# A softmax that streams 128 row groups through one core: the last four of six 15-row loads issued as two 30-row loads

## Chip, cores, metric

The kernel runs on one core of a Trainium2 chip. The metric is device time in microseconds (us), median of three runs. One core has five engines with their own instruction streams (TensorE, VectorE, ScalarE, GpSimd, SyncE; in the profile PE, DVE, ACT, POOL, SP) and 16 DMA engines that all DMA queues share. A DMA that is issued by SP, ACT or POOL goes to a queue of that issuer; the profile calls SP's queue q1, ACT's q10 and POOL's q0.

## The reference

```python
x: (16, 1024, 512) float32
x_scaled = x / 2.0
exp_x = np.exp(x_scaled - max(x_scaled, axis=-1))
return exp_x / sum(exp_x, axis=-1)        # softmax over the last 512
```

16384 rows of 512 floats are read once and written once: 33.55 MB in, 33.55 MB out.

## The kernel before

The rows are taken as 128 row groups ("rows" from here on): a row is 512 floats on each of 128 partitions, 0.262 MB. The 128 rows are cut into ten tiles, listed in `TILES` (L10) as (rows, place in the arena): 3, 5, and eight times 15. The tile numbers 0 to 9 are positions in this list. A tile of r rows is laid out so that partition p holds r neighbouring rows of DRAM: with r = 15 that is one run of 30720 bytes per partition.

The data live in one SBUF buffer, `arena` (L49), of 98 rows. Tiles 0 to 7 fill it (3 + 5 + 6 x 15 = 98). Tiles 8 and 9 reuse the places of rows 0 to 29: tile 8 those of tiles 0, 1 and 2 (the first 15 rows), tile 9 those of tiles 2 and 3. `LATE` (L14) writes this down: the load of tile 8 waits for the stores of tiles 0, 1 and 2, the load of tile 9 for that of tile 3.

Everything is done in place, and each engine runs through the tiles in order:

- **Loads.** SP loads tile 0, ACT tile 1 (`early`, L155), ACT then tiles 2 to 7 one behind the other with no wait between them (`loads`, L159). POOL loads tiles 8 and 9 (L178 to L181): it waits until the exponentials of all rows below row 83 are done (`TURN`, L22; that is the end of tile 6), then for the stores named in `LATE`.
- **Release to ACT.** PE waits for each tile's load in order and raises `s_go` by the number of chunks in the tile (L195, L196). A chunk is 5 rows, the first one 3.
- **Exponentials.** ACT takes one unit of `s_go` for a chunk (L142), then runs one ACTIVATE per row: exp(x/2) with the sum of the row into `stats` (L206, L275). The maximum is not subtracted; a check of the sums at the end (L182 to L192) sets a flag, and only if a sum is outside of its limits does a slow path recompute everything (`rounds`, L144).
- **Normalising.** DVE takes the reciprocal of the sums (L168) and multiplies the tile by it (L171): one pair of instructions for each 15-row tile, for the last tile one per 5 rows. `upto[t]` is the number of multiplications after which tile t is ready.
- **Stores.** SP stores the tiles in order (L213 to L216), each after its multiplication (L135). Tile 1 (`SPREAD`, L20) is stored in three DMAs (`pieces`, L116): four of its five rows on 128 partitions (8192 bytes each), the fifth row on 126 partitions (2048 bytes each), and the fifth row on the last two partitions. Before the store of tile 2, SP waits until all pieces of tiles 0 and 1 have landed (L215): 64 on the semaphore `s_home[8]`.

So the order of transfers is set by three queues (ACT's loads, SP's stores, POOL's two late loads), each in the order of issue, and by how the DMA engines share themselves between the queues.

Of the kernel before, what the change touches and what calls it, by code (L numbers as in the profile page):

```python
# [10 lines left out]
    (3, 0), (5, 3), (15, 8), (15, 23), (15, 38), (15, 53), (15, 68), (15, 83), (15, 0), (15, 15),  # L11
]

LATE = {8: (0, 1, 2), 9: (3,)}  # L14
ARENA = 98

HEAD = [3]
# [2 lines left out]
SPREAD = 1  # L20
# [8 lines left out]
def kernel(  # L29
# [5 lines left out]
    nc = tc.nc  # L35
# [6 lines left out]
    xf = x.flatten_outer_dims()  # L42
    of = out.flatten_outer_dims()
    N, D = xf.shape
    P = nc.NUM_PARTITIONS
# [14 lines left out]
    tiles, base = [], 0  # L60
# [2 lines left out]
        tiles.append((base, r, at))  # L63
        base += r

    def dram(ap, t):
        b, r, _ = tiles[t]
        return ap[b * P : (b + r) * P].rearrange("(p r) d -> p r d", r=r)

    def sb(t):  # L70
        _, r, at = tiles[t]
        return arena[:, at : at + r, :]

    straight = sum(HEAD)
# [3 lines left out]
    owner = [max(t for t, (b, _, _) in enumerate(tiles) if b <= s) for s in starts]  # L78
# [9 lines left out]
            pairs.append([k])  # L88
    upto = [1 + max(j for j, ks in enumerate(pairs) if owner[ks[0]] == t) for t in range(len(tiles))]

    ld = [nc.alloc_semaphore(f"ld{t}") for t in range(len(tiles))]
    s_home = {t: nc.alloc_semaphore(f"s_home{t}") for t in LATE}
    s_near = nc.alloc_semaphore("s_near")
    s_end = nc.alloc_semaphore("s_end")
    s_exp = nc.alloc_semaphore("s_exp")
    s_go = nc.alloc_semaphore("s_go")
    s_rec = nc.alloc_semaphore("s_rec")
    s_mul = nc.alloc_semaphore("s_mul")
# [11 lines left out]
    g_rec = nc.alloc_semaphore("g_rec")  # L110
    g_mul = nc.alloc_semaphore("g_mul")

    def load(eng, t):
        eng.dma_start(out=sb(t), in_=dram(xf, t)).then_inc(ld[t], 16)  # L114

    def pieces(t):  # L116
        r = tiles[t][1]
        if t == SPREAD:
            return [(0, P, 0, r - 1), (0, 126, r - 1, r), (126, P, r - 1, r)]
        return [(0, P, 0, r)]  # L120

    stored_by = {u: s_home[t] for t, us in LATE.items() for u in us}
    for t, (_, r, at) in enumerate(tiles):
        over = {u for u, (_, ru, au) in enumerate(tiles[:t]) if at < au + ru and au < at + r}
        assert over <= {u for v, us in LATE.items() if v <= t for u in us}

    def landings(ts):
        return 16 * sum(len(pieces(t)) for t in ts)

    near = len(tiles) - 2  # L130
    sem_of = {**stored_by, near: s_near}
    at_end = landings(t for t in range(len(tiles)) if t not in sem_of)

    def store(eng, t):
        eng.wait_ge(s_mul, upto[t])  # L135
        for p, q, lo, hi in pieces(t):
            eng.dma_start(
                out=dram(of, t)[p:q, lo:hi], in_=sb(t)[p:q, lo:hi]
            ).then_inc(sem_of.get(t, s_end), 16)

    def take(eng, sem, n):
        eng.wait_ge(sem, n).then_inc(sem, -n)  # L142

    def rounds(eng, body):  # L144


        i = eng.alloc_register("general")
        eng.wait_ge(s_near, 16)
        eng.wait_ge(s_flag, 1)
        eng.reg_load(i, flag[0:1, 0:1])  # L150
        with eng.While(lambda: eng.snap(i, min_val=0, max_val=1) < 1):
            body()
            eng.reg_add(i, i, 1)

    def early():  # L155
        load(nc.sync, 0)
        load(nc.scalar, 1)

    def loads():  # L159
        for t in range(2, min(LATE)):  # L160
            load(nc.scalar, t)

    def program():

        for j, ks in enumerate(pairs):
            b, c = starts[ks[0]], sum(sizes[k] for k in ks)
            a = b % ARENA
            nc.vector.reciprocal(  # L168
                out=recip[:, b : b + c], in_=stats[:, b : b + c]
            )._wait_ge(s_exp, ks[-1] + 1).then_inc(s_rec, 1)  # L170
            nc.vector.tensor_mul(  # L171
                out=arena[:, a : a + c],
                in0=arena[:, a : a + c],
                in1=recip[:, b : b + c].unsqueeze(2).to_broadcast([P, c, D]),
            )._wait_ge(s_rec, j + 1).then_inc(s_mul, 1)

        nc.gpsimd.memset(ones[:, :], 1.0).then_inc(s_ones, 1)  # L177
        nc.gpsimd.wait_ge(s_exp, starts.index(TURN))  # L178
        for t, us in LATE.items():
            nc.gpsimd.wait_ge(s_home[t], landings(us))  # L180
            load(nc.gpsimd, t)  # L181
        nc.gpsimd.tensor_scalar(  # L182
            out=inside[:, :], in0=stats[:, :], scalar1=LO, scalar2=HI,
            op0=Alu.max, op1=Alu.min,
        )._wait_ge(s_exp, len(sizes)).then_inc(s_cnt, 1)
        nc.vector.scalar_tensor_tensor(  # L186
            out=inside[:, :], in0=inside[:, :], scalar=1.0, in1=stats[:, :],
            op0=Alu.mult, op1=Alu.is_equal, accum_out=count[:, :],
        )._wait_ge(s_cnt, 1).then_inc(s_cnt, 1)
        nc.vector.tensor_scalar(  # L190
            out=flag[:, :], in0=total[:, :], scalar1=float(N), scalar2=None, op0=Alu.is_ge,
        )._wait_ge(s_tot, 1).then_inc(s_flag, 1)  # L192


        for t in range(len(tiles)):  # L195
            nc.tensor.wait_ge(ld[t], 16).then_inc(s_go, owner.count(t))  # L196
        nc.tensor.wait_ge(s_ones, 1)
        nc.tensor.matmul(  # L198
            total[:, :], lhsT=count[:, :], rhs=ones[:, :], start=True, stop=True
        )._wait_ge(s_cnt, 2).then_inc(s_tot, 1)  # L200

        nc.scalar.preload_act_table(Exp)  # L202
        for k, c in enumerate(HEAD):
            take(nc.scalar, s_go, 1)
            for b in range(starts[k], starts[k] + c):
                ins = nc.scalar.activation(  # L206
                    out=arena[:, b], in_=arena[:, b], func=Exp, scale=0.5,
                    accum_out=stats[:, b : b + 1],
                )
            ins.then_inc(s_exp, 1)  # L210
        exponentials(straight, n_rows)

        for t in range(len(tiles)):  # L213
            if t == SPREAD + 1:
                nc.sync.wait_ge(s_home[min(LATE)], landings(range(t)))  # L215
            store(nc.sync, t)  # L216

        x_g = xf.rearrange("(t p r) d -> t p r d", p=P, r=G)  # L220
        o_g = of.rearrange("(t p r) d -> t p r d", p=P, r=G)
        data = arena[:, 0:G]

        def vector():
            for i in range(n_rows // G):
                nc.vector.reduce_max(
                    out=g_max[:, :], in_=data, axis=mybir.AxisListType.X, negate=True
                )._wait_ge(g_go, i + 1).then_inc(g_top, 1)
                nc.vector.reduce_sum(
                    out=g_sum[:, :], in_=data, axis=mybir.AxisListType.X  # L230
                )._wait_ge(g_exp, i + 1).then_inc(g_add, 1)
                nc.vector.reciprocal(
                    out=g_sum[:, :], in_=g_sum[:, :]
                )._wait_ge(g_add, i + 1).then_inc(g_rec, 1)

        def scalar():
            for i in range(n_rows // G):
                nc.scalar.activation(out=data, in_=data, func=Exp, scale=0.5)._wait_ge(
                    g_sub, i + 1
                ).then_inc(g_exp, 1)  # L240

        def gpsimd():
            nc.gpsimd.wait_ge(s_end, at_end)
            for i in range(n_rows // G):
                nc.gpsimd.dma_start(out=data, in_=x_g[i]).then_inc(g_ld, 16)
                nc.gpsimd.wait_ge(g_ld, 16 * (i + 1)).then_inc(g_go, 1)
                nc.gpsimd.tensor_add(
                    out=data, in0=data, in1=g_max[:, :].unsqueeze(2).to_broadcast([P, G, D])
                )._wait_ge(g_top, i + 1).then_inc(g_sub, 1)
                nc.gpsimd.tensor_mul(  # L250
                    out=data, in0=data, in1=g_sum[:, :].unsqueeze(2).to_broadcast([P, G, D])
                )._wait_ge(g_rec, i + 1).then_inc(g_mul, 1)
                nc.gpsimd.wait_ge(g_mul, i + 1)
                nc.gpsimd.dma_start(out=o_g[i], in_=data).then_inc(g_st, 16)
                nc.gpsimd.wait_ge(g_st, 16 * (i + 1))

        rounds(nc.vector, vector)
        rounds(nc.scalar, scalar)
        rounds(nc.gpsimd, gpsimd)
        nc.sync.wait_ge(s_near, 16)  # L260
        nc.sync.wait_ge(s_end, at_end)
# [26 lines left out]
    first = list(entry.instructions)  # L288
    at = next(k for k, i in enumerate(head) if type(i).__name__ == "InstDrain")
    entry.instructions = head[:at] + first + head[at:]  # L290
    act = []
    entry.instructions = list(entry.instructions) + [i for i in jumps if i not in act]
    nc.switch_body(here, parent=None, valid_engines=[i.engine for i in jumps])
    loads()
    program()


# [28 lines left out]
```

## Time and profile before

| | us |
|---|---|
| median of 3 runs (159.81 to 159.98) | 159.98 |
| the profiled execution | 159.75 |
| its span in the profile | 158.4 |
| ACT busy, of the span | 80.6 |
| DVE busy, of the span | 73.2 |
| last DVE instruction ends | 129.4 |
| bytes moved | 67.11 MB, 424 GB/s over the span |

The profiled execution took 0.23 us less than the median of the runs and 1.35 us more than its own span. All times in the text below are microseconds from the span's start. The profile also records single DMA packets: on this kernel one packet is the run of one partition in a DMA (30720 bytes for a 15-row tile), and each DMA has 8 of them on each of the 16 engines, followed on each engine by a 4-byte packet that reports completion.

### The profile page before, as it was taken

What the parts mean: (1) busy time and instruction counts of PE and PEld (TensorE: products, weight loads), DVE (VectorE), ACT (ScalarE), POOL (GpSimd) and SP (SyncE); (2) the same over time, 40 slices, a digit from 0 to 9 for tenths busy, and PEclk for the clock granted to TensorE, in tenths of its full rate; (3) what the DMA queues carried; (4) which work ended last, traced back from release to release, by engine and by line L of the source; (5) the groups of instructions that cost most, each with busy time, mean ns of one, the idle gap of its engine ahead of it and who ended that gap; (6) DMA issues with size and microseconds to landing.
All of it is one profiled execution on the core that took longest, in us unless ns stands there. A gap on an engine that the chain in (4) does not pass through costs nothing. (4 is left out here: it accounts for less than half of the span.)

```text
span 158.4 us, 658 instructions
## 1 busy us (share of the span) xinstructions
PE 0.2 (0%) x2; PEld 0.1 (0%) x2; DVE 73.2 (46%) x27; ACT 80.6 (51%) x257; POOL 2.2 (1%) x8
## 2 busy tenths in 40 slices
PE   0000000000000000000000000000000000000000
PEld 0000000000000000000000000000000000000000
DVE  0066000992994979903970029808927960000000
ACT  0780399598899980795005971991059700000000
POOL 0000000000000000001000010000000100000000
DMA  7999998999999999999898989898989898989896
GB/s 270 469 411 383 461 439 357 446 470 412 395 502 389 442 427 427 442 411 458 388 481 380 489 380 489 380 489 380 489 372 496 372 489 380 489 380 489 380 481 264
DMA packets 3024, 67.11 MB, mean 424 GB/s; under 512 B 336, under 2 KB 336, under 8 KB 720
## 3 DMA queue, kind: packets, MB, share of 16 engines
q1 hardware_dynamic: 1728, 34.34, 50.7%
q10 hardware_dynamic: 1008, 24.90, 37.0%
q0 software_dynamic: 288, 7.86, 11.5%
HBM read 33.55 MB, written 33.55 MB: 424 GB/s over the span
## 5 line engine op out<-in xcount | busy, mean ns | idle before, releaser
L275 ACT ACTIVATE arena<-arena x125 | 76.7, 615 | 40.2 <-ACTq L142 40.2
L171 DVE TENSOR_TENSOR arena<-arena,recip 128x7680 f32<-128x7680 f32 (+2 forms) x12 | 70.2, 5847 | 0.4
L168 DVE RECIPROCAL recip<-stats 128x15 f32<-128x15 f32 (+2 forms) x12 | 2.7, 224 | 55.5 <-ACT arena L275 47.3
L275 ACT ACTIVATION_READ_ACCUMULATOR arena<-arena x125 | 23.4, 187 | 0.0
L202 ACT ACT_TABLE_LOAD x1 | 1.3, 1283 | 5.0 <-issue 5.0
L114 POOL DMA_DIRECT2D arena<-in_x_dram x2 | 1.3, 631 | 90.3 <-ACT arena L275 72.3
L206 ACT ACTIVATE arena<-arena 128x512 f32<-128x512 f32 x3 | 1.9, 618 | 0.0
L182 POOL TENSOR_SCALAR inside<-stats 128x128 f32<-128x128 f32 x1 | 0.6, 631 | 32.6 <-ACT arena L275 32.6
L206 ACT ACTIVATION_READ_ACCUMULATOR arena<-arena 128x1 f32 x3 | 0.6, 185 | 0.0
L198 PE MATMUL total<-ones,count 128*1 128x1 f32 x2 | 0.2, 164 | 129.1 <-DVE inside L186 129.1
L186 DVE SCALAR_TENSOR_TENSOR inside<-inside,stats 128x128 f32<-128x128 f32 x1 | 0.3, 284 | 0.0
L190 DVE TENSOR_SCALAR flag<-total 1x1 int32<-1x1 f32 x1 | 0.1, 147 | 0.3 <-PE total L198 0.3
L198 PEld LDWEIGHTS total<-ones,count 128*1 128x1 f32 x2 | 0.1, 80 | 129.1 <-DVE inside L186 129.1
L177 POOL MEMSET ones<- 128x1 f32 x1 | 0.1, 99 | 1.1 <-POOLq L37 1.1
L310 POOL MEMSET const-float32-0.0<- 128x1 f32 x1 | 0.1, 105 | 0.2 <-issue 0.2
L310 POOL MEMSET const-bfloat16-1.0<- 128x1 bf16 x1 | 0.1, 108 | 0.0
L310 POOL MEMSET const-uint8-127<- 128x1 uint8 x1 | 0.1, 108 | 0.0
L310 POOL MEMSET const-float32-1.0<- 128x1 f32 x1 | 0.1, 105 | 0.0
L186 DVE DVE_READ_ACCUMULATOR inside<-inside,stats 128x1 f32 x1 | 0.1, 83 | 0.0
## 6 DMA issues: line engine op xcount, KB each, us to landing
out_dram<-arena SPq DMA_DIRECT2D x8, 3840.0 KB, 42.9
arena<-in_x_dram ACTq DMA_DIRECT2D x6, 3840.0 KB, 41.7
arena<-in_x_dram POOLq DMA_DIRECT2D x2, 3840.0 KB, 23.7
arena<-in_x_dram ACTq DMA_DIRECT2D x1, 1280.0 KB, 7.3
out_dram<-arena SPq DMA_DIRECT2D x1, 1024.0 KB
arena<-in_x_dram SPq DMA_DIRECT2D x1, 768.0 KB, 5.9
out_dram<-arena SPq DMA_DIRECT2D x1, 768.0 KB
out_dram<-arena SPq DMA_DIRECT2D x1, 252.0 KB
```

The source lines that it names most:

```text
L114: eng.dma_start(out=sb(t), in_=dram(xf, t)).then_inc(ld[t], 16)
L168: nc.vector.reciprocal(out=recip[:, b : b + c], in_=stats[:, b : b + c])._wait_ge(s_exp, ks[-1] + 1).then_inc(s_rec, 1)
L171: nc.vector.tensor_mul(out=arena[:, a : a + c], in0=arena[:, a : a + c], in1=recip[:, b : b + c].unsqueeze(2).to_broadcast([P, c, D]),)._w ...
L177: nc.gpsimd.memset(ones[:, :], 1.0).then_inc(s_ones, 1)
L182: nc.gpsimd.tensor_scalar(out=inside[:, :], in0=stats[:, :], scalar1=LO, scalar2=HI, op0=Alu.max, op1=Alu.min,)._wait_ge(s_exp, len(sizes) ...
L186: nc.vector.scalar_tensor_tensor(out=inside[:, :], in0=inside[:, :], scalar=1.0, in1=stats[:, :], op0=Alu.mult, op1=Alu.is_equal, accum_ou ...
L190: nc.vector.tensor_scalar(out=flag[:, :], in0=total[:, :], scalar1=float(N), scalar2=None, op0=Alu.is_ge,)._wait_ge(s_tot, 1).then_inc(s_f ...
L198: nc.tensor.matmul(total[:, :], lhsT=count[:, :], rhs=ones[:, :], start=True, stop=True)._wait_ge(s_cnt, 2).then_inc(s_tot, 1)
L202: nc.scalar.preload_act_table(Exp)
L206: ins = nc.scalar.activation(out=arena[:, b], in_=arena[:, b], func=Exp, scale=0.5, accum_out=stats[:, b : b + 1],)
L275: ins = nc.scalar.activation(out=data, in_=data, func=Exp, scale=0.5, accum_out=stats[:, r : n_rows - E + 1 + r][:, bass.ds(now, 1)],)
L310: nc = _bacc.Bacc("TRN2", target_bir_lowering=False, num_devices=1)
```

## The change

The list of tiles stays, but what one load and one store cover is now listed apart from it. `LOADS` puts tiles 4 and 5 into one load and tiles 6 and 7 into one load; `STORES` has one store per tile as before. In a 30-row load, partition p holds 30 neighbouring rows of DRAM: one run of 61440 bytes, of which tile 4 is the first half and tile 5 the second. The stores of tiles 4 to 7 still move 15 rows, 30720 bytes per partition, now with a step of 61440 bytes in DRAM between partitions.

With it, the semaphores `ld` are one per load; PE waits for a load and releases all chunks of both its tiles at once (six instead of three). ACT issues five loads instead of seven. `LATE` is renumbered by loads (tile 8 is load 6, tile 9 load 7); what the late loads wait for, the chunks, the multiplications, the pieces of tile 1 and the order on SP stay as they were.

```diff
-LATE = {8: (0, 1, 2), 9: (3,)}
+LOADS = [(0,), (1,), (2,), (3,), (4, 5), (6, 7), (8,), (9,)]
+STORES = [(0,), (1,), (2,), (3,), (4,), (5,), (6,), (7,), (8,), (9,)]
+
+LATE = {6: (0, 1, 2), 7: (3,)}
...
-    def dram(ap, t):
-        b, r, _ = tiles[t]
-        return ap[b * P : (b + r) * P].rearrange("(p r) d -> p r d", r=r)
-
-    def sb(t):
-        _, r, at = tiles[t]
+    def span(ts):
+        assert all(tiles[u][2] == tiles[t][2] + tiles[t][1] for t, u in zip(ts, ts[1:]))
+        return tiles[ts[0]][0], sum(tiles[t][1] for t in ts), tiles[ts[0]][2]
...
+    blocks = [span(ts) for ts in LOADS]
+
+    def dram(ap, ts):
+        b, r, _ = span(ts)
+        first, rows, _ = next(blocks[k] for k, us in enumerate(LOADS) if ts[0] in us)
+        assert first <= b and b + r <= first + rows
+        block = ap[first * P : (first + rows) * P].rearrange("(p r) d -> p r d", r=rows)
+        return block[:, b - first : b - first + r]
+
+    def sb(ts):
+        _, r, at = span(ts)
         return arena[:, at : at + r, :]
...
-    def load(eng, t):
-        eng.dma_start(out=sb(t), in_=dram(xf, t)).then_inc(ld[t], 16)
...
+    def load(eng, k):
+        eng.dma_start(out=sb(LOADS[k]), in_=dram(xf, LOADS[k])).then_inc(ld[k], 16)
...
-    def store(eng, t):
-        eng.wait_ge(s_mul, upto[t])
-        for p, q, lo, hi in pieces(t):
+    def store(eng, j):
+        ts = STORES[j]
+        eng.wait_ge(s_mul, upto[ts[-1]])
+        for p, q, lo, hi in pieces(j):
             eng.dma_start(
-                out=dram(of, t)[p:q, lo:hi], in_=sb(t)[p:q, lo:hi]
-            ).then_inc(sem_of.get(t, s_end), 16)
+                out=dram(of, ts)[p:q, lo:hi], in_=sb(ts)[p:q, lo:hi]
+            ).then_inc(sem_of.get(j, s_end), 16)
...
     def loads():
-        for t in range(2, min(LATE)):
-            load(nc.scalar, t)
+        for k in range(2, min(LATE)):
+            load(nc.scalar, k)
...
-        for t in range(len(tiles)):
-            nc.tensor.wait_ge(ld[t], 16).then_inc(s_go, owner.count(t))
+        for k, ts in enumerate(LOADS):
+            nc.tensor.wait_ge(ld[k], 16).then_inc(
+                s_go, sum(owner.count(t) for t in ts)
+            )
...
-        for t in range(len(tiles)):
-            if t == SPREAD + 1:
-                nc.sync.wait_ge(s_home[min(LATE)], landings(range(t)))
-            store(nc.sync, t)
+        for j in range(len(STORES)):
+            if j == SPREAD + 1:
+                nc.sync.wait_ge(s_home[min(LATE)], landings(range(j)))
+            store(nc.sync, j)
```

More of the change, by code (lines that the diff above doesn't have):

```diff
@@ L64 @@
         base += r
-    def dram(ap, t):
-        b, r, _ = tiles[t]
-        return ap[b * P : (b + r) * P].rearrange("(p r) d -> p r d", r=r)
-    def sb(t):
-        _, r, at = tiles[t]
+    def span(ts):
+        assert all(tiles[u][2] == tiles[t][2] + tiles[t][1] for t, u in zip(ts, ts[1:]))
+        return tiles[ts[0]][0], sum(tiles[t][1] for t in ts), tiles[ts[0]][2]
+    for part in (LOADS, STORES):
+        assert [t for ts in part for t in ts] == list(range(len(tiles)))
+    blocks = [span(ts) for ts in LOADS]
[7 more added lines that the diff above has]
+        _, r, at = span(ts)
         return arena[:, at : at + r, :]
@@ L89 @@
     upto = [1 + max(j for j, ks in enumerate(pairs) if owner[ks[0]] == t) for t in range(len(tiles))]
-    ld = [nc.alloc_semaphore(f"ld{t}") for t in range(len(tiles))]
-    s_home = {t: nc.alloc_semaphore(f"s_home{t}") for t in LATE}
+    ld = [nc.alloc_semaphore(f"ld{k}") for k in range(len(blocks))]
+    s_home = {k: nc.alloc_semaphore(f"s_home{k}") for k in LATE}
     s_near = nc.alloc_semaphore("s_near")
@@ L111, with pieces, landings @@
     g_mul = nc.alloc_semaphore("g_mul")
-    def load(eng, t):
-        eng.dma_start(out=sb(t), in_=dram(xf, t)).then_inc(ld[t], 16)
-    def pieces(t):
-        r = tiles[t][1]
-        if t == SPREAD:
+    def load(eng, k):
+        eng.dma_start(out=sb(LOADS[k]), in_=dram(xf, LOADS[k])).then_inc(ld[k], 16)
+    def pieces(j):
+        r = span(STORES[j])[1]
+        if STORES[j] == (SPREAD,):
             return [(0, P, 0, r - 1), (0, 126, r - 1, r), (126, P, r - 1, r)]
         return [(0, P, 0, r)]
[L122 to L130, printed above, removed]
-    sem_of = {**stored_by, near: s_near}
-    at_end = landings(t for t in range(len(tiles)) if t not in sem_of)
-    def store(eng, t):
-        eng.wait_ge(s_mul, upto[t])
-        for p, q, lo, hi in pieces(t):
+    stored_by = {j: s_home[k] for k, js in LATE.items() for j in js}
+    for k, (_, r, at) in enumerate(blocks):
+        over = {
+            j for j, ts in enumerate(STORES)
+            if ts[0] < LOADS[k][0] and span(ts)[2] < at + r and at < span(ts)[2] + span(ts)[1]
+        }
+        assert over <= {j for v, js in LATE.items() if v <= k for j in js}
+    def landings(js):
+        return 16 * sum(len(pieces(j)) for j in js)
+    near = len(STORES) - 2
+    sem_of = {**stored_by, near: s_near}
+    at_end = landings(j for j in range(len(STORES)) if j not in sem_of)
+    def store(eng, j):
+        ts = STORES[j]
+        eng.wait_ge(s_mul, upto[ts[-1]])
+        for p, q, lo, hi in pieces(j):
             eng.dma_start(
-                out=dram(of, t)[p:q, lo:hi], in_=sb(t)[p:q, lo:hi]
-            ).then_inc(sem_of.get(t, s_end), 16)
+                out=dram(of, ts)[p:q, lo:hi], in_=sb(ts)[p:q, lo:hi]
+            ).then_inc(sem_of.get(j, s_end), 16)
     def take(eng, sem, n):
@@ L178, in program @@
         nc.gpsimd.wait_ge(s_exp, starts.index(TURN))
-        for t, us in LATE.items():
-            nc.gpsimd.wait_ge(s_home[t], landings(us))
-            load(nc.gpsimd, t)
+        for k, js in LATE.items():
+            nc.gpsimd.wait_ge(s_home[k], landings(js))
+            load(nc.gpsimd, k)
         nc.gpsimd.tensor_scalar(
```

## The prediction, on record before the result

> **What bounds the kernel now.** I read the page first: nothing computes for more than 51% of the span, and the DMA row is at 9 or 8 almost throughout. The sums over stretches say it more exactly (columns: PE, PEld, DVE, ACT and POOL busy, then PE's clock, the DMA engines' mean busy share, GB/s):
>
> ```profile
> PE 0.2 (0%) x2; PEld 0.1 (0%) x2; DVE 73.2 (46%) x27; ACT 80.6 (51%) x257; POOL 2.2 (1%) x8
> ```
> ```profile
> 2.00:28.00 26.00, 0.00 (x0) 0.00 (x0) 5.32 (x6) 15.58 (x47) 0.00 (x0) 1.00 1.02 423
> 28.00:49.00 21.00, 0.00 (x0) 0.00 (x0) 16.44 (x3) 18.15 (x59) 0.00 (x0) 1.00 1.02 436
> 49.00:85.00 36.00, 0.00 (x0) 0.00 (x0) 25.23 (x6) 19.24 (x63) 0.73 (x1) 1.00 1.00 432
> 85.00:130.00 45.00, 0.19 (x2) 0.09 (x2) 26.22 (x13) 27.65 (x90) 1.17 (x2) 1.00 1.00 430
> 130.00:157.00 27.00, 0.00 (x0) 0.00 (x0) 0.00 (x0) 0.00 (x0) 0.00 (x0) 1.00 1.01 437
> ```
>
> From 2 to 157 us all 16 DMA engines are busy, and for the last 27 us they only store. The time is therefore the bytes' time plus whatever the DMA engines idle. The chain of waits and the compute engines set nothing as long as some queue has packets.
>
> The second reading is how the engines share themselves out. A stretch in which ACT's queue loads 30720-byte packets and SP's queue stores the 8192-byte packets of tile 1:
>
> ```profile
> q10 hardware_dynamic: 79, 2.43, 79.1%
> q1 hardware_dynamic: 79, 0.65, 21.5%
> ```
>
> That is 28.9 to 36 us: 79 packets against 79, whatever their size. Each engine serves one packet of one queue, then one of the other. So a store packet costs its own time and the time of one load packet, and **a longer load packet slows every store beside it**. The completion packets take turns too, as the packet records show.
>
> The third is SP. Its waits, and its instructions from 48 to 54 us:
>
> ```profile
> SPq L137 <- DMA out_dram<-arena: 13.0, 1, 13.0
> ```
> ```profile
> 49.08 0.84 SPq L137 DMA_DIRECT2D out_dram<-arena  x2
> ```
>
> For 13 us SP has tiles 2 and 3 ready or nearly so (multiplied by 36.0 and 47.3) but waits for tile 1's pieces to land; then it issues both stores. From 48.6 to 52.9 no store packet is served: the load queue alone fills the engines.
>
> ```profile
> DMA packets 54, 1.57 MB, mean 364 GB/s; under 512 B 3, under 2 KB 3, under 8 KB 3
> ...
> q10 hardware_dynamic: 54, 1.57, 87.2%
> ```
>
> **Part 1, packets: a small saving.** A 10240-byte packet takes 385 ns and a 30720-byte one 1138 ns in the records: 36.8 ns per 1000 bytes and 8.5 ns fixed. The four loads have 32 packets per engine, now 16: 16 x 8.5 ns = 0.14 us, and two completion packets fewer at 9 ns, together 0.15 us off the DMA time. A 61440-byte packet is estimated at 1138 + 30720 x 36.8/1000 = 2268 ns, 1.13 us more than now. No row shows such a packet; the bounds are two turns of 30720 bytes (a rival below) and one turn.
>
> The Trainium skill, "DMA: Bandwidth & Descriptors", gives each DMA about 2 us fixed (Anatomy of one DMA) and asks for few large ones; two DMAs fewer would be an estimated 4 us by that. The packet records speak against it here: the last packet of tile 3's load ends at 27.6 and tile 4's first starts at 27.91, the gap holding a store packet, so queued loads have no fixed cost to save.
>
> **Part 2, turns: when the store chain of tile 1 ends.** I count on one of the two DMA engines that carry the two-partition piece. Tile 4's first load packet starts at 27.91. Behind it the store queue has five 8192-byte packets, a completion, nine 2048-byte packets, a completion, and the extra 2048-byte packet with its completion: 17 turns. The load queue has tile 4's 8 packets, a completion and tile 5's 8 packets: 17 turns. So the extra packet follows the last data packet of tile 5, which the records confirm: tile 5's last packets end at 48.3 to 48.8, the extra ones are at 48.42 and 48.43, their completion is done at 48.52. Today that is halfway: tiles 6 and 7 are queued behind.
>
> With the change the same 17 load turns are block (4, 5), a completion and block (6, 7): **the whole rest of the load queue**. The turn count is unchanged, each of the 16 data turns is 1.13 us longer, 18.1 us in sum. The extra packet's completion is done at 48.52 + 18.07 = 66.59, and the loads end at 66.39 to 66.87, mean 66.6. At that moment both queues are empty: tiles 2 and 3, long multiplied, wait on SP for tile 1's landing; tile 8's load waits on POOL for tile 2's store and for the rows of tile 6, which have only just arrived.
>
> **Part 3, the hole.** Today from the last completion (48.52) to SP's issue (49.08) it takes 0.56 us: SP issues at 67.15. From an issue to the first packets there are two sorts of rows. On idle DMA engines: tile 0's load, issued at 0.00, first packets at 1.00 to 1.53. Beside loads: tile 2's store, 49.08 to 53.0; tile 0's store, 10.22 to 14.15; there the packet waits behind load packets. At 67.15 the engines are idle, so I take the first row: first packets at 68.15 to 68.68, mean 68.4. All 16 engines idle for 68.4 - 66.6 = **1.8 us**. The lower end is 1.3 (earliest start against latest end, 68.15 - 66.87); the upper end from the loaded rows, 3.9 instead of 1.25 from issue, is 4.5. Today's cover, the queued loads of tiles 6 and 7, is gone.
>
> **Part 4, what else moves, at nothing.** ACT issues two loads fewer (some 0.6 us each, 4.80 for seven), so its table load (4.95 to 6.23) moves up and the first exponential can start when tile 0 is released at 6.02 instead of 6.25: at most 0.2 us, into a DMA-bound stretch. PE's release of tile 4 moves from 39.8 to about 48.3 (block landing: 27.91 + 8 x 2.26 + small store packets 1.7 + 0.4); exponentials of 15 rows take 9.2, a multiplication 8.2 and 0.3 for the reciprocal, so tile 4 is ready near 66.3, tile 5 near 75.6, and with the second block landing near 67.2, tile 6 near 85 and tile 7 near 94. After the hole tiles 2 and 3 keep the engines busy to 68.4 + 2 x 9.1 = 86.6, tile 4 is queued behind: no second hole. Tile 2's store lands near 78, the rows of tile 6 are done at 76.7, so POOL issues tile 8's load near 78 (now 73.94) with packets from 82; with the 4 turns of tile 3 that remain at 82 POOL issues tile 9's load near 93 (now 92.7); its data lands near 119 (now 116.1). The last multiplication ends near 132 (now 128.8), with some 28 us of stores still queued. POOL's delays are hidden by those stores.
>
> **Sum.** Against the profiled execution: 159.75 + 1.8 - 0.15 = 161.4, span 160.05. It was 0.23 below the median, so a median of 159.98 + 1.65 = **161.6**. Its own range takes the hole from 1.3 to 2.9 (halfway to the loaded end): 161.1 to 162.7.
>
> **Rivals.**
>
> *The packet is cut.* If the 61440 bytes are served as two packets of 30720, the turns are today's: tile 1 lands at 49, no hole there. Tiles 6 and 7 are released only at 84, and POOL loads tile 8 after 93 instead of 74; stores of tiles 3 to 5 fill 82 to 98, as tiles 4 and 5 are multiplied by 67 and 76. Time 159.9 to 160.0. For it: no 61440-byte packet in the trace. Against: each partition's run was one packet in all sizes from 2048 to 30720. The Trainium skill's same page (SWDGE vs HWDGE vs iDMA) puts a packet at 4096 bytes preferably; the 30720-byte records disagree, but a limit above them is not shown. Chance 0.11.
>
> *The store chain ends one turn earlier.* The count of part 2 is a dead heat. Tile 0's store may go out up to 0.2 us sooner (part 4); if that brings both critical engines one turn forward of 1.13 us (about 0.2/1.13, less as both must), the extra packet follows the last load packet but one, SP issues near 65, and tile 2's first packet arrives under the last load packet: no hole, 159.83. Chance 0.11.
>
> *Slow first packets.* If an issue into empty queues takes as long as one beside loads (3.9), the hole is 4.5: 159.98 + 4.5 - 0.15 = 164.3. For it: ACT's first load took 2.4 (0.12 to 2.51). Against: that one had tile 0's load in front of it. Chance 0.07.
>
> *A real gain.* Without a hole, and if the engines' ends draw together (final completions spread from 157.40 to 157.94) by 0.3: 159.5. Against: nothing in the profile ties the two together. Chance 0.06.
>
> **How the numbers follow.** Forecast 0.65. A difference of 0.2%, 0.32 us, is about what a measurement of this kernel can tell from none. Slower: forecast and slow first packets, 0.72. Same: cut packet and earlier turn, 0.22. Faster: 0.06. The range runs from the no-hole cases (159.83, less a little) to the forecast's own upper end: 159.7 to 162.7, which leaves out the slow first packets and most of the gain.
>
> **What would show it.** In the changed profile: load packets of 61440 bytes at about 2.27 us; SP's issue of tile 2 at 67 instead of 49; a stretch near 66.6 to 68.4 with the DMA row near nothing and full rows on both sides; from 69 to the end no other gap, and the last DVE instruction near 132. It is wrong if ACT's queue still has 30720-byte packets for tiles 4 to 7, if SP issues tile 2 before the last load packet starts (64), or if the hole lies elsewhere.

## The result and the profile after

The changed kernel takes 162.40 us (median of 5 runs, 162.11 to 162.41) against 159.91 us: 1.0154 times as long, 95% interval 1.0140 to 1.0168. The profiled execution took 162.41 us with a span of 161.1, 2.7 more than the span before. The prediction said 161.6, slower, for an empty-queue hole; the hole is there, but it is not the whole difference.

SP's waits and its instructions from 66 to 69 us, in the changed kernel:

```profile
SPq L155 <- DMA out_dram<-arena: 31.4, 1, 31.4
```
```profile
67.07 1.80 SPq L155 DMA_DIRECT2D out_dram<-arena  x3
```

SP waited 31.4 us for tile 1's pieces to land, 13.0 before, and then issued the stores of tiles 2, 3 and 4 one behind the other at 67.07 instead of 49.08. Tiles 2 and 3 had long been ready, and tile 4 became ready at 66.8, while it waited. The packets of all queues in the microsecond around that issue, 66.9 to 67.9:

```profile
DMA packets 0, 0.00 MB, mean 0 GB/s; under 512 B 0, under 2 KB 0, under 8 KB 0
```

And the stretches after it (columns as in the prediction: the last two are the DMA engines' mean busy share and GB/s):

```profile
66.00:68.50 2.50, 0.00 (x0) 0.00 (x0) 1.72 (x3) 2.50 (x9) 0.00 (x0) 1.00 0.47 198
68.50:82.00 13.50, 0.00 (x0) 0.00 (x0) 12.68 (x3) 13.50 (x45) 0.73 (x1) 1.00 1.02 437
82.00:94.00 12.00, 0.00 (x0) 0.00 (x0) 11.22 (x3) 3.89 (x14) 0.53 (x1) 1.00 0.98 369
94.00:130.00 36.00, 0.00 (x0) 0.00 (x0) 13.83 (x7) 17.63 (x57) 0.00 (x0) 1.00 1.01 436
```

The first line is the predicted hole: half of the DMA time between 66 and 68.5 is empty. The third line was not predicted. From 82 to 94 us the engines are busy for 0.98 of the time, yet they move 369 GB/s where the stretches beside it move 437 and 436, and where the kernel before moves 428 in the same stretch:

```profile
82.00:94.00 12.00, 0.00 (x0) 0.00 (x0) 0.11 (x1) 9.22 (x30) 0.54 (x1) 1.00 0.99 428
```

**A busy engine is not an engine at its rate**: the packet records of that stretch show 38 packets of 30720 bytes, of 144, that took 1400 to 2240 ns instead of 1138 (called stretched below). Added up over all packets of this size from 80 to 104 us, the time beyond 1138 ns is 1.60 us per DMA engine, against 0.02 in the kernel before. The first 16 of them, as many as there are engines, are store packets that start at 82.84 to 82.98 and end as the first packets of POOL's load start (84.57 to 85.10); the rest are packets of POOL's loads.

The DMA queues show that the packets are as the change says. After, and then ACT's queue before:

```profile
DMA packets 2736, 67.11 MB, mean 417 GB/s; under 512 B 304, under 2 KB 304, under 8 KB 688
...
q10 hardware_dynamic: 720, 24.90, 36.1%
```
```profile
q10 hardware_dynamic: 1008, 24.90, 37.0%
```

ACT's queue carries the same 24.90 MB in 720 packets instead of 1008. The 512 packets of tiles 4 to 7 became 256 of 61440 bytes, and the completions of two DMAs (32) are gone: 1008 - 256 - 32 = 720. Each 61440-byte packet took 2267 ns.

### The profile page after: what moved, and what is told of

It reads as the page before. It is cut to its first block, busy times and chain, and to the rows that moved or that the text cites. A ratio compares the mean times of both kernels' runs of the same rounds, so it can differ in the third digit from the quotient of the medians.

```text
span 161.1 us, 654 instructions
## 1 busy us (share of the span) xinstructions
PE 0.2 (0%) x2; PEld 0.1 (0%) x2; DVE 73.2 (45%) x27; ACT 80.4 (50%) x257; POOL 2.2 (1%) x8
## 3 DMA queue, kind: packets, MB, share of 16 engines
q10 hardware_dynamic: 720, 24.90, 36.1%
```

## The experiments

Times of the table are medians; each ratio is against runs of the kernel before on the same chip. "Empty" says whether all queues ran empty before tile 2's store. "Stretched" is worked out from each run's packet records: the time beyond 1138 ns of the 30720-byte packets that start from 80 to 104 us, per DMA engine. "Ends" are the first and last of the 16 DMA engines' final completions in the profile.

| kernel | us | ratio, 95% interval | empty | stretched, us | ends |
|---|---|---|---|---|---|
| before | 159.91 | | no | 0.02 | 157.4 to 157.9 |
| changed | 162.40 | 1.0140 to 1.0168 | yes | 1.60 | 160.4 to 160.7 |
| e1 tile 1 in one store | 161.75 | 1.0110 to 1.0139 | no | 0.94 | 158.0 to 160.1 |
| e2 no wait on SP | 160.36 | 1.0020 to 1.0044 | no | 0.01 | 157.5 to 160.7 |
| e3 only (4, 5) | 160.10 | 1.0001 to 1.0018 | no | 0.01 | 157.7 to 158.5 |
| e4 before, wait for tile 7's load | 162.87 | 1.0183 to 1.0210 | yes | 1.56 | 160.7 to 161.0 |
| e5 only (6, 7) | 160.60 | 1.0028 to 1.0060 | no | 0.57 | 157.8 to 159.1 |
| e6 changed, POOL's load later | 162.43 | 1.0141 to 1.0172 | yes | 1.51 | 160.4 to 160.8 |
| e7 before, POOL's load later | 160.07 | 1.0007 to 1.0037 | no | 0.01 | 157.4 to 157.9 |
| e8 before, no wait on SP | 166.70 | 1.0398 to 1.0438 | no | 0.27 | 157.3 to 165.2 |
| e10 changed, other wait on SP | 160.98 | 1.0056 to 1.0080 | no | 0.12 | 157.7 to 159.0 |

The eight runs of e2 lie between 160.10 and 164.19 us, and its profiled execution took 162.36, well above the median, so its ends are those of a long run. e9 is told apart below. The window of the column "stretched" does not hold all stretched packets of a run; those before it are told in the section on stretched packets.

### Is it the wait, or the long packets?

**e4** makes the meeting of the queues without long packets: the kernel before, all loads 30720 bytes, with one wait more on SP.

```diff
             if t == SPREAD + 1:
                 nc.sync.wait_ge(s_home[min(LATE)], landings(range(t)))
+                nc.sync.wait_ge(ld[min(LATE) - 1], 16)
```

> The kernel before, all packets 30720 bytes, but SP also waits for the landing of tile 7's load before it stores tile 2. It makes the changed kernel's meeting without its packets: queues empty near 66.6, SP issues near 67. Empty-queue theory: 161.4 for the hole alone, 162.5 with the stretched packets at POOL's first load (0.15 more than the changed kernel, which saves packets). Rival, the loss needs 61440-byte packets: about 160.

```profile
67.44 1.80 SPq L137 DMA_DIRECT2D out_dram<-arena  x3
```
```profile
66.00:68.50 2.50, 0.00 (x0) 0.00 (x0) 1.72 (x3) 2.50 (x10) 0.00 (x0) 1.00 0.47 197
```

The loads end at 67.0, SP issues at 67.44, the first store packets start at 68.30, and the time is 162.87 us. The whole loss, hole and stretched packets, appears without one long packet. So the loss does not need long packets; what they do in the changed kernel is to delay tile 1's store until nothing is left behind it. That they cost nothing by themselves is not shown: the kernels below that keep a pair and have no hole, with tile 1 stored as before, are 0.25 to 1.1 us slower than the kernel before.

**e3** pairs only tiles 4 and 5, so that the turns of tile 1's store end with tile 6's load, while tile 7's is still queued.

```diff
-LOADS = [(0,), (1,), (2,), (3,), (4, 5), (6, 7), (8,), (9,)]
+LOADS = [(0,), (1,), (2,), (3,), (4, 5), (6,), (7,), (8,), (9,)]
-LATE = {6: (0, 1, 2), 7: (3,)}
+LATE = {7: (0, 1, 2), 8: (3,)}
```

> Only tiles 4 and 5 are loaded as a pair, 6 and 7 singly. Empty-queue theory: the 17 turns now end with the load of tile 6, 8 x 1.13 = 9 us later than in the kernel before; SP issues tile 2's store near 58 us while tile 7's load is still queued, no hole, 159.8. ACT's loads end near 71 us and POOL's load 8 begins near 80: in between stores are alone, so if joining a store-only stream stretches packets, 160.5 to 161.1. Rival, the cost is proportional to the long packets: half of the 2.5 us, 161.2, with the loss before 66 us.

```profile
58.22 0.83 SPq L155 DMA_DIRECT2D out_dram<-arena  x2
```

SP issues at 58.22, 9.1 us later than before: 8 turns of 1.13 us, as counted. No hole, no stretched packets where POOL's load joins, 160.10 us, 0.25 us above the kernel before on the same chip.

**e5** pairs only tiles 6 and 7 (the same two lines, with `(4,), (5,), (6, 7)`).

> Only tiles 6 and 7 are loaded as a pair, 4 and 5 singly. Empty-queue theory: tile 1's store chain ends with tile 5's load at 48.5 as in the kernel before, SP issues tile 2's store at 49 us, the long packets are queued behind it, no hole and no stretched packets at POOL's first load: 159.8 (half of the packet saving, 0.08), at most 0.3 more for packets stretched where tile 2's store joins. Rival, long packets cost by themselves: 161.

```profile
49.15 0.84 SPq L155 DMA_DIRECT2D out_dram<-arena  x2
```

SP's issue is where it was before, there is no hole, and the time is 160.60 us: more than expected, less than the rival. The 0.57 us of stretched packets and DMA engines that end 1.3 us apart instead of 0.5 are about as much. Neither pair gave a gain.

### Is it a dead heat of turns?

**e1** stores tile 1 in one DMA, which takes 12 turns out of the chain on two engines (nine 2048-byte packets, the extra one, and two completions; the expectation counts 11) and 10 on most others.

```diff
-        if STORES[j] == (SPREAD,):
-            return [(0, P, 0, r - 1), (0, 126, r - 1, r), (126, P, r - 1, r)]
         return [(0, P, 0, r)]
```

> The changed kernel with both pairs, but tile 1 stored in one DMA (eight 10240-byte packets and a completion) instead of three. Empty-queue theory: the store chain of tile 1 now has 11 turns fewer on the two engines with the two-partition piece and 10 on most others, so it ends some 23 us before the last load packet; SP issues tile 2's store near 45 us, no stretch without packets near 67, time 159.8 (159.91 less 0.15), or up to 0.4 more because the fifth row's uneven spread over the engines is gone; if the 1.3 us of stretched packets at 82 to 94 us belong to the hole they are gone too, if they belong to POOL's load joining a store-only stream they stay and the time is near 161. Rival, long packets or the 61440-byte step of the stores cost the time by themselves: 162.4 as before.

SP issues tile 2's store at 44.8 and there is no hole, but the time is 161.75 us, much more than expected. Two things keep it up: stretched packets, 0.94 us in the table's window and 0.63 earlier, most of it in load packets that start at 46 to 49 us, and the DMA engines' ends, from 158.0 to 160.1, 2.1 us apart. The uneven ends cost more than the 0.4 us that I gave them; that the missing fifth-row piece is the reason is not shown, as e5 and e10 keep the piece and end 1.3 and 1.2 us apart. The run shows that the hole goes away with the turns; it does not show the time without a hole.

**e2** leaves out SP's wait.

```diff
-            if j == SPREAD + 1:
-                nc.sync.wait_ge(s_home[min(LATE)], landings(range(j)))
             store(nc.sync, j)
```

> The changed kernel with both pairs, without SP's wait for the landing of tiles 0 and 1 before it stores tile 2. Empty-queue theory: tile 2's store is issued at 36 us and its packets stand in SP's queue when the last load packet ends at 66.6; no hole. Time 159.8 if the stretched packets at 82 to 94 us came with the hole, 160.5 to 161.1 if they come whenever POOL's load joins a stream of stores alone. Rival, the long packets cost it by themselves: 162.4.

160.36 us: 2.0 less than the changed kernel, with one wait less. No hole, and no stretched packets from 80 to 104 us. **e10** keeps a wait, but one that ends at 48.6:

```diff
-                nc.sync.wait_ge(s_home[min(LATE)], landings(range(j)))
+                nc.sync.wait_ge(ld[4], 16)
```

> The changed kernel with both pairs, but SP holds tile 2's store until block (4, 5) has landed (about 48.5 us) instead of until tiles 0 and 1 have been stored. If the hole is only a matter of when SP issues, tile 2's packets stand behind tile 1's pieces when the last load packet ends at 66.6, no packet-free stretch follows, the stretched packets at 80 to 104 us are gone (430 GB/s there, not 410), and the time is 159.8 to 160.4; the upper end if the DMA engines end as unevenly as in the runs with one pair. If it stays above 161.5, the wait was not the cause.

```profile
66.00:68.50 2.50, 0.00 (x0) 0.00 (x0) 1.72 (x3) 1.41 (x6) 0.00 (x0) 1.00 0.98 419
80.00:104.00 24.00, 0.00 (x0) 0.00 (x0) 16.82 (x4) 14.46 (x48) 1.27 (x2) 1.00 1.00 428
```

The stretch that was half empty is full, and the later one moves 428 GB/s. The time, 160.98 us, is above the expected 160.4: two DMA engines end at 158.8 and 159.0, the other 14 by 158.2.

**e8** is the control: the kernel before without SP's wait.

> The kernel before, without SP's wait for the landing of tiles 0 and 1 before it stores tile 2. Control for the same edit on the changed kernel: queued loads hide that wait here, so 159.9, within 0.3. If it is slower by about as much as the changed kernel without the wait (0.5), that remainder comes from the missing wait and not from the pairs.

166.70 us, a miss by 7. The DMA records of its last stretch, 158.5 to 165.4:

```profile
DMA packets 12, 0.31 MB, mean 45 GB/s; under 512 B 2, under 2 KB 2, under 8 KB 2
...
q1 hardware_dynamic: 12, 0.31, 10.3%
```

Two DMA engines still have five packets each, and their completions, when 14 have ended by 158. With the packets chained end to start, these two engines lost about 6.5 us to stretched packets, most others 1 to 2. They are ahead of the others at tile 2's store (its completions at 56.5 on two engines, at 65.5 on most). So the wait does more in the kernel before than hold stores back: with it the 16 engines end within 0.5 us of each other, without it 7.9 us apart. Why two engines out of step are slowed is not shown by these runs.

### What stretches the packets at 82 to 94 us?

**e6** moves POOL's load in the changed kernel, **e7** in the kernel before; both by one line.

```diff
-TURN = 83
+TURN = 98
```

> The changed kernel, with POOL's load of tile 8 held back until the rows of tile 7 are done (near 86 us instead of 78). The hole at 66.5 to 68 us stays. If the stretched packets come from the hole, which starts all 16 DMA engines within 0.15 us of each other so that POOL's load meets all of them at once, they move with the load, to 90 us and later, and the time stays at 162.4 within 0.4. If they come from what else runs at 82 to 94 us, they stay there or are gone, and with the hole alone the time is 161.3.

> The kernel before, with POOL's load of tile 8 held back until the rows of tile 7 are done (near 94 us). ACT's loads end at 84, so POOL's load joins stores alone, without a hole before. If stretching needs the hole: none, and about 160.0. If it comes from joining a stream of stores alone: about 1 us per engine near 98 us, time 161.

The stretch from 80 to 104 us, first e6, then e7, then the changed kernel, then the kernel before:

```profile
80.00:104.00 24.00, 0.00 (x0) 0.00 (x0) 13.72 (x3) 6.03 (x20) 1.26 (x2) 1.00 1.01 408
```
```profile
80.00:104.00 24.00, 0.00 (x0) 0.00 (x0) 10.47 (x3) 9.29 (x30) 1.27 (x2) 1.00 1.00 430
```
```profile
80.00:104.00 24.00, 0.00 (x0) 0.00 (x0) 13.59 (x3) 6.38 (x21) 0.53 (x1) 1.00 1.02 410
```
```profile
80.00:104.00 24.00, 0.00 (x0) 0.00 (x0) 10.52 (x3) 15.05 (x49) 0.54 (x1) 1.00 1.00 430
```

In e6 POOL issues at 86.33, and in the records nearly all packets over 1.3 us start at 91.1 to 91.2 us and at 101.0 to 101.3 instead of at 82.8 to 84.8 and 90.5 to 93.4: they moved with the load. In e7 POOL's load joins stores alone, at 97.3, and nothing is stretched. So neither the time of day nor a store-only stream does it by itself. In this window it is 1.5 to 1.6 us in the table's three kernels with a hole, and 0.01 to 0.94 in the eight without one.

The two rows for 82 to 94 us above differ in one more thing: VectorE is busy for 11.22 us there in the changed kernel and for 0.11 in the kernel before. The same row of e3, where POOL's load joins at 82.0 and nothing is stretched, shows that VectorE's work alone does not do it:

```profile
82.00:94.00 12.00, 0.00 (x0) 0.00 (x0) 11.22 (x3) 4.19 (x14) 0.53 (x1) 1.00 0.98 425
```

Nor does stretching need a hole or POOL's load. The packet records outside the window show it where a store comes to loads that had the engines to themselves. In the kernel before, 12 load packets at 51.7 to 53.1 us took 1.20 to 1.50 us, about when tile 2's store starts (53.0): 0.14 us per engine. In e3, 24 load packets at 59.7 to 61.4 took up to 2.12 us, before tile 2's store starts at 62.3: 0.53 us. In e2 and e10 most of the 61440-byte packets that tile 2's store meets near 64 to 67 took 2.5 us and more, up to 3.3 in e2: 0.52 and 0.62 us per engine beyond 2267 ns. e1, without a hole, comes to 1.57 us in its two places together, as much as the changed kernel at POOL's load. So part of what these kernels lose against the kernel before is stretching too.

**e9** asked whether it is that the hole starts all 16 engines in step (their last store packets before POOL's first load packet start within 0.14 us in the changed kernel, within 0.4 in e7 and 1.1 in e3). It cuts tile 2's store.

```diff
+        if STORES[j] == (2,):
+            return [(0, P, 0, 7), (0, 120, 7, r), (120, P, 7, r)]
         return [(0, P, 0, r)]
```

> The changed kernel, hole included, with tile 2's store cut into three DMAs: seven rows on 128 partitions, then eight rows on 120 partitions and on 8. A 16384-byte packet is estimated at 0.6 us from the packet rows, so after it some eight of the 16 DMA engines stand half a packet behind seven others when POOL's first load arrives, where they were within 0.15 us before. If the stretched packets at 82 to 94 us come from all engines meeting the load at the same instant, their sum (1.4 us per engine) falls to 0.7 or less; if they only need the hole, or something else that runs then, it stays between 1.2 and 1.5. The engines end more unevenly by one such packet, so the whole time may be 162 to 163 either way and decides nothing.

The edit broke more than the step. The time is 170.58 us, and from 80 to 84 us, where the two cut pieces are stored, the records show packets of up to 4.0 us:

```profile
DMA packets 52, 0.86 MB, mean 216 GB/s; under 512 B 16, under 2 KB 16, under 8 KB 16
```

It decides nothing on the question: 1.46 us are stretched from 80 to 104, but a part of that is the pieces' own. Whether engines in step are the cause stays open. Against it: in e1 the last store packets start 1.15 us apart, and 0.94 us are stretched all the same.

## Why the prediction was right

Its range held the time, and the direction was right. The mechanism was right for the hole, 1.5 us of the loss; the size was 0.8 us short (1.65 forecast, 2.49 measured), because another 1.6 us came from a cost that it put at nothing. That the range held is in part luck: its upper end, 162.7, stood for a hole of 2.9 us, and what filled the range was not a longer hole. By its steps:

- **Packets (part 1).** A 61440-byte packet took 2267 ns, 2268 estimated. It is one turn, so the rival of the cut packet fell. The saving of 0.15 us is there in the packets' own time, hidden under what follows.
- **Turns (part 2).** Tile 1's last completion was done at 66.49 (66.59 forecast), the loads ended at 66.36 to 66.80 (66.39 to 66.87). The count of turns gave the end of the chain, but it did not hold to the turn on every engine: the second DMA of tile 1 completed at 64.1 to 64.5 on nine engines of 14 and at 66.4 to 66.5, one load packet later, on five, where the kernel before has 47.2 to 47.7 on all 14. As the load queue was at its end, a turn later cost nothing; a turn earlier on both critical engines would have been the prediction's rival without a hole. That the slip went the harmless way is luck. Tile 0's store did not go out sooner but later, at 10.55 instead of 10.22: tile 0's load landed later, and the freed ACT waited for it.
- **The hole (part 3).** From the last completion to SP's issue 0.58 us (0.56 forecast); from issue to first packets 0.85 to 1.00 us (1.00 to 1.53 taken from tile 0's load). Hence 1.5 us idle on average over the 16 engines instead of 1.8. The idle row was the right one to take; the loaded rows, 3.9, were queued load packets. (The prediction's row of 364 GB/s for 48.6 to 52.9 counts packets by their start, three rounds where almost four fit. Chained end to start, its packets leave no engine idle there.)
- **No second loss (part 4). This is the step that failed.** The order was right: POOL issued at 78.23 and 91.67 (78 and 93 forecast), tiles 4 to 7 were ready at 66.8, 76.0, 85.2 and 94.4 (66.3, 75.6, 85, 94; the sum for tile 4's release adds up to 48.1 and not to 48.3, and its first exponential started at 49.0), the last multiplication ended at 134.0 (132), the queues never ran empty again. But I priced every packet after the hole at its usual time, and 1.6 us per engine went to stretched packets when POOL's load joined; why they stretch is open. POOL's first packet started at 84.57, 6.3 us after its issue, 4.2 before.

The sum with measured terms: 1.5 for the hole, 1.6 less 0.02 for stretched packets, 0.15 less for fewer packets, 2.9. The 16 engines' final completions moved by 2.87 on average, the span by 2.7, as they end closer together now (0.3 instead of 0.5 us apart).

The Trainium skill's rule of few large DMAs ("DMA: Bandwidth & Descriptors", Rules for kernel authors) bought nothing here, as the queues' gaps before the change said. The prediction's estimate of 4 us does not fit the case either: the Trainium skill fits its 2 us per DMA (the same page, Anatomy of one DMA) to DMAs issued from GpSimd, and the paired loads are issued by ACT. The Trainium skill's rule that an engine serves the queue rows in turn by packets (the same page, Queues, rings and completion order) is the one that the prediction read from the trace, and the packet records of the kernel before and of the changed one agree with it, with packets of 2048 to 61440 bytes in one turn each.

## What to carry to other kernels

In a kernel like this one, whose DMA engines are always busy, a change of the loads has little to gain, but it can lose cover: ask which transfers are queued at the moment when an issuing engine's wait ends, and count that in turns, not in bytes. Making packets of one queue longer slows each packet of the other queue by the difference, so a wait on a chain of small stores grows with the packet size of the loads beside it. After an idle stretch, and where a queue joins, look at GB/s as well as at busy shares: the engines can be busy and slow.

## What the runs showed of the hardware

- An SP store into empty queues has its first packets 0.85 to 1.00 us after the issue; the same store beside loads 3.9.
- A hole of 1.5 to 1.7 us per engine was followed in the changed kernel, e4 and e6 by 1.5 to 1.6 us of stretched packets when POOL's load joined (in e9, whose cut pieces are stretched themselves, 1.46). The cause is open.
- Without a hole, packets were stretched by 0.14 to 0.62 us per engine in the kernel before, e2, e3 and e10 where tile 2's store came to loads that had run alone.
- Unevenness between DMA engines matters at the end: their ends lie within 0.5 us in the kernel before; with tile 1 in one store, after the change, they were 2.1 us apart, and without SP's wait, in the kernel before, 7.9.
- Cutting a store into 120 and 8 partitions gave packets of up to 4.0 us.
